# A three-pass fp32 backbone step: tanh gates, first sums on VectorE, and a pipeline for the right rows of two norms

## The chip, the cores and the metric

One core of a Trainium2 chip. The metric is the device time of one execution in microseconds (us), as the median of several runs. The engines named below are TensorE (PE in profile rows, PEld for its weight loads), VectorE (DVE), ScalarE (ACT), GpSimd (POOL) and SyncE (SP), whose queue starts most DMAs. Each engine works through its own queue in order.

## The reference

One layer of a diffusion backbone, for 128 context tokens and 512 latent tokens, width 1024, SwiGLU width 2816, four mLSTM heads of 256:

```python
mod = silu(cond) @ w_mod + b_mod
sh1, sc1, g1, shm, scm, gm, sh2, sc2, g2 = split(mod, 9)
h = modulate(rmsnorm(x, norm_g[0]), sh1, sc1)
x = x + 0.5 * g1 * swiglu(h, ffn1_w1, ffn1_w2)        # (silu(a) * b) @ w2
h = modulate(rmsnorm(x, norm_g[1]), shm, scm)
y, C, n, m = mixer(h, ...)
x = x + gm * y
h = modulate(rmsnorm(x, norm_g[2]), sh2, sc2)
x = x + 0.5 * g2 * swiglu(h, ffn2_w1, ffn2_w2)
...
# mixer
z = h @ w_in + b_in
q, k, v = heads of z;  o = sigmoid(z[O])
hm = mlstm_bidir(q, k, v, i, f, state)                # chunks of 128 tokens, two directions
hm = hm * rsqrt(mean(hm * hm) + EPS) * ml_norm
ml = (o * hm) @ w_ml_out
sc = (b * conv3(c * x)) @ w_sc_out
y = sigmoid(z[GML]) * ml + sigmoid(z[GSC]) * sc
return y @ w_o, C, n, m
```

At the end comes one more RMSNorm. `modulate(h, sh, sc)` is `h * (1 + sc) + sh`.

## The kernel before

**Products.** Activations are kept transposed (features on partitions), the 640 tokens in two halves of 320. Each fp32 product is three products of rounded parts, hi·hi, hi·lo and lo·hi (`three`, L240 to L242). `split` (L72 to L74) makes the parts: ScalarE casts hi, VectorE subtracts it to leave lo. Weights arrive by SyncE's DMAs (`w_load`, L197) in a ring of five raw tiles (`wr`).

**Pairs.** Most weights are used two tiles of 128 columns at a time, against the two halves of the tokens, by a form of Strassen's product with seven products instead of eight (`pair_el`, `pair_steps`). It goes through A11, S1, S2, A12, S3, S4, A22 in that order, and each meets activations of its own: H11, HT1, HT2, H21, HT3, H22, HT4. S1 to S4 are sums and differences of weight tiles (`ws`, L213): S2 and S4 are always VectorE's, S1 and S3 are those of the engine `e1`. Ahead of the last product, VectorE at L289 takes a copy of the accumulator plus the S1 product, since A22 (against HT4) then goes on adding in the same accumulator: HT4's first product waits for L289. A queue of casts runs four operations ahead of TensorE. In the first feed-forward part's first three pairs, `e1` is GpSimd.

**Norms and heads.** The last group of the matmuls ahead of norm two (ffn1's second product) and norm three (the mixer's output product) adds to the residual x (`add_x`, L844), squares it on ScalarE (L713), and VectorE adds the squares up in `sqacc` (L717). Half 0 of the tokens (the left rows) is then normalised while half 1 is still worked on: `left_lists` deals out, after each step of that group, lists of small works: `sc_` (scale by the norm, `scale_x`, VectorE, L760), `md` (`modulate`, L768 on ScalarE or L770 on VectorE), `sp` (`split` into H11 for k=0 to 3 and H21 for k=4 to 7). k counts the eight 128-row tiles of the width.

`head_el` then runs the next matmuls' first three column blocks on half 0, tile by tile: k=0 to 3 with H11, 4 to 7 with H21. Between them stands the statistics of half 1 (the right rows), made by `right_chain`: `chain[0]` sums the squares over partitions (L735), takes root and reciprocal and puts the result on a diagonal (L745); `chain[1]` spreads it (L752) and scales and modulates; `chain[2]` and `chain[3]` modulate and split the rest. Between the halves stand a few adaLN units (L561). Half 1 then reads HT4 for k=0 to 3 (a tile that the pairs use for something else later) and H22 for k=4 to 7.

**Gates.** Gate o is made in `q_pair` (L1325), per head; gml in `gml_pair` (L1532), for the first branch (mLSTM), and is written out by a GpSimd DMA; gsc, for the second branch, at L1655. All are Sigmoid on ScalarE. The attention weights between them use Exp (`w_exp`, L1344). Where two neighbouring functions are in different tables, an ACT_TABLE_LOAD stands between them. `r_out` (L1479) multiplies the transposed mLSTM output by ml_norm and o and writes it to DRAM (`rd`); `r_in` reads it and splits it (Bh, Bl); `ml_ev` (L1633) multiplies the first branch's product by gml, and `sc_ev` (L1673, L1674) the second's by gsc, and adds the two. In the scan, L1370, L1391 and L1437 are ScalarE's copies, L1407 scales an output, and the context state Cc goes out by DMA.

Orders are static: the program's order on each engine is the order of execution.

Of the kernel before, what the change touches and what calls it, by code (L numbers as in the profile page):

```python
# [7 lines left out]
F32 = mybir.dt.float32  # L8
# [4 lines left out]
P = 128  # L13
# [31 lines left out]
def mixer_step(ctx: ExitStack, tc: tile.TileContext, x_prompt, x_sample, state_C, state_n, state_m,  # L45
# [285 lines left out]
    def head_el(blocks, chain, work, mid=()):  # L331
# [7 lines left out]
        def emit():  # L339
# [22 lines left out]
            for k in range(KT):  # L362
                if k == 4:
                    for t in range(3):
                        w[t].append(op())
                for t in range(3):
                    three(ps[t][:, :HT], *w[t][k // 4], k % 4, plain_acts(k, 0), k == 0, k == KT - 1)
                if k == 3:
                    chain[0]()
                if k == 4:  # L370
                    chain[1]()
# [404 lines left out]
    def left_lists(n, sh):  # L776
        sc_ = lambda *ks: [lambda k=k: scale_x(0, k, N["rb", 0]) for k in ks]
        md = lambda *ks: [lambda k=k: modulate(0, k, n, sh, "AAV"[k % 3]) for k in ks]
        sp = lambda *ks: [lambda k=k: put("11" if k < 4 else "21", k % 4, N[0, k]) for k in ks]
        return [[stat_fn(0)], [rows_fn(0)] + sc_(0, 1, 2), sc_(3, 4) + md(0, 1), sc_(5, 6) + md(2) + sp(0),  # L780
                sc_(7) + md(3, 4) + sp(1, 2), md(5, 6) + sp(3, 4), md(7) + sp(5, 6, 7)]

# [11 lines left out]
    def right_chain(n, sh):  # L794
# [6 lines left out]

        def scales():
            for k in range(KT):
                scale_x(1, k, N["rb", 1])

        def mods(ks):
            for k in ks:
                modulate(1, k, n, sh, "AV"[k % 2])

        def right(ks):  # L810
            for k in ks:
                if k < 4:
                    HB.setdefault("12", [None] * 4)[k] = hl = hpair("T4")
                    split(N[1, k], *hl)
                else:
                    put("22", k - 4, N[1, k])

# [10 lines left out]
        def t4(k):  # L828
# [6 lines left out]
        last = [lambda k=k: put("T4", k, N["T", k]) for k in ks]  # L835
        chain = [stat_fn(1), all_of(rows_fn(1), scales, lambda: mods(range(4))),
                 all_of(lambda: mods(range(4, 8)), lambda: right(range(4))), lambda: right(range(4, 8))]
        return chain + last, work

# [57 lines left out]
    def after_lists(n, sh):  # L897
        lists = left_lists(n, sh)

        def after(h, i):  # L900
            if h == 1:
                for f in lists[i]:
                    f()
                if i == 5:
                    for f in lists[6]:
                        f()
        return after
# [200 lines left out]
    ptr["cap"] = 0  # L1108
    head, els = ffn(ffn1_w1, ffn1_w2, G1, after_lists(1, SHM), first_head, G)
    prog += [head] + with_units(els[0][0], mod_units(G1)) + [step(lambda: relax(0)), step(half_gate(G1))]  # L1110
# [200 lines left out]
    def q_pair(h, nm_, off):  # L1311
        S = HD[h]

        def ev(mi, hf, src):
            col0 = off + h * DH + mi * P
            if hf == 0 or (nm_, mi) not in S:
                if nm_ in "qk":
                    S[nm_, mi] = xp.tile([P, T], F32, name="x", bufs=KT)
                else:
                    S[nm_, mi] = PO["h1"].tile([P, T], F32, name=nm_, bufs=2)  # L1320
            dst = S[nm_, mi][:, hsl(hf)]
            if nm_ == "k":
                V.tensor_scalar(dst, src, bias(col0), DH ** -0.5, op0=OP.add, op1=OP.mult)
            else:
                A.activation(dst, src, AF.Sigmoid if nm_ == "o" else AF.Identity, bias=bias(col0))  # L1325
        return z_load(off + h * DH), z_load(off + h * DH + P), ev
# [20 lines left out]
    def head_steps(h):  # L1347
# [122 lines left out]
        def r_out(dt):  # L1470
            def f():
                j = 2 * h + dt
                for c0, c1 in ((0, 2), (2, NCH)):
# [4 lines left out]
                    o = S["o", dt][:, a:a + n]  # L1478
                    V.scalar_tensor_tensor(o, p[:, :n], col("ml", j), o, op0=OP.mult, op1=OP.mult)  # L1479
                G.dma_start(rd[j], S["o", dt])  # L1480
# [48 lines left out]
    def gml_pair(m):  # L1529
        def ev(mi, h, src):  # L1530
            t = t3()
            A.activation(t, src, AF.Sigmoid, bias=bias(GML_OFF + (m + mi) * P))  # L1532
            G.dma_start(gd[m + mi][:, hsl(h)], t)
        return z_load(GML_OFF + m * P), z_load(GML_OFF + (m + 1) * P), ev
# [3 lines left out]
    def cx_pair(m):  # L1538
        def ev(mi, h, src):
# [25 lines left out]
            for o, i in segs:  # L1565
# [6 lines left out]
                        mod_mid(GM, 0)))  # L1572
    prog += [step(spill_x), step(close_u), step(open_h1)]
    gate, NG = gates(), 38
# [40 lines left out]
    def r_in(j):  # L1615
        def f():
            for h in range(2):
                RB[j, h] = bpair()
                split(RT[j][:, hsl(h)], *RB[j, h])
        return f  # L1620
# [9 lines left out]
    def ml_ev(m):  # L1630
        def ev(h, ps):
            t = GM_T[m][:, hsl(h)]
            V.tensor_mul(t, ps, t)  # L1633
            if h == 1:
                G.dma_start(td[m], GM_T[m])
# [196 lines left out]
```

## Time and profile before

| | before |
|---|---|
| runs, us | 1711.39, 1711.75, 1712.96; median 1711.75 |
| profiled execution | 1712.5, of it span 1710.7 |
| busy, share of the span | TensorE 98%, VectorE 74%, ScalarE 47%, GpSimd 10% |
| mean granted TensorE clock | 0.997 |
| 0 to about 165 us | adaLN, norm one, ffn1's first pairs |
| 492 to 519 us | norm two and the mixer's head |
| 606 to 870 us | the scan and the gates o and gml |
| 1256 to 1280 us | norm three and ffn2's head |

A row of the timeline reads: start, duration, engine, line, operation, output <- inputs, shape, and in brackets how long the engine had been idle and what ended that. A row of groups ends with busy time and mean ns of one, then the idle time ahead of it. A row of waits gives total, times and longest.

### The profile page before, as it was taken

To read this page: it belongs to the slowest core of one execution; us is meant where nothing else is said; L and a number is where in the kernel's file an instruction comes from. 1 tells how busy PE (TensorE), PEld (TensorE's weight loads), DVE (VectorE), ACT (ScalarE), POOL (GpSimd) and SP (SyncE) were. 2 spreads that over 40 slices of the span, in tenths; PEclk is the share of its full clock that TensorE was granted. 3 is DMA by queue.
4 is the path that set the end of the run, shared out by engine and by line. 5 is a ranking of instruction groups with operands and counts; after the bars stand their busy time and mean duration, and the time that the engine had idled before them with its cause. 6 is when DMAs were issued, how large, how long until landed. Compare 5 with 4: busy or idle time off the path is not lost.

```text
span 1710.7 us, 29505 instructions
## 1 busy us (share of the span) xinstructions
PE 1669.3 (98%) x11275; PEld 1622.8 (95%) x11275; DVE 1268.8 (74%) x2677; ACT 798.4 (47%) x1719; POOL 166.3 (10%) x250
## 2 busy tenths in 40 slices
PE   7999999999999899999999999999999999999998
PEld 4979999999989899999999999999989999999997
DVE  6757786886778867777887788869677567567476
ACT  4542452542556666465652355542265335245243
POOL 2010000000030231111111212011100000000002
PEclk9999999999999999999999999999999999999999
DMA  9344334333352443333348423357432322323221
GB/s 310 87 150 135 99 110 122 109 109 107 106 155 75 107 105 84 84 100 83 94 140 265 131 75 87 95 164 215 132 99 65 97 62 84 91 75 87 87 75 62
DMA packets 277245, 193.14 MB, mean 113 GB/s; under 512 B 12147, under 2 KB 255226, under 8 KB 277104
## 3 DMA queue, kind: packets, MB, share of 16 engines
q1 hardware_dynamic: 268592, 162.62, 33.0%
q0 software_dynamic: 8480, 28.63, 6.0%
q8 instruction: 89, 1.46, 0.4%
q14 instruction: 52, 0.43, 0.1%
q10 hardware_dynamic: 32, 0.01, 0.0%
HBM read 175.92 MB, written 15.31 MB: 112 GB/s over the span
## 4 chain that ended last, share of the span: by engine, by line
PE 83%; DVE 8%; ACT 5%; issue 3%; DMA 1%; POOL 0%; ACTq 0%; DVEq 0%; POOLq 0%
PE ps L240 25%; PE ps L242 25%; PE ps L241 25%; DVE wl L74 2%; PE ax L1401 1%; PE ax L1432 1%; ACT wh L73 1%; PE ax L636 1%; PE ax L1404 1%; DVE ws L213 1%; DVE t L1545 1%; DMA wr<-in_ffn_w_dram 1%; PE ax L561 0%; DVE x L1557 0%; PE ax L1378 0%
## 5 line engine op out<-in xcount | busy, mean ns | idle before, releaser
L74 DVE TENSOR_TENSOR wl<-wr,wh 128x512 fp32r<-128x512 f32 (+1 forms) x410 | 268.1, 669 | 80.4 <-ACT wh L73 78.7
L73 ACT CAST wh<-wr 128x512 fp32r<-128x512 f32 (+1 forms) x410 | 238.6, 593 | 181.7 <-PE ps L241 152.6
L74 DVE TENSOR_TENSOR wl<-ws,wh 128x512 fp32r<-128x512 f32 x288 | 202.5, 704 | 62.8 <-ACT wh L73 62.4
L73 ACT CAST wh<-ws 128x512 fp32r<-128x512 f32 x288 | 175.2, 618 | 112.6 <-DVE ws L213 66.0
L240 PE MATMUL ps<-Uh,wh 128*128 128x320 f32 x704 | 218.8, 311 | 0.0
L241 PE MATMUL ps<-Ul,wh 128*128 128x320 f32 x704 | 217.6, 309 | 0.0
L242 PE MATMUL ps<-Uh,wl 128*128 128x320 f32 x704 | 217.4, 309 | 0.0
L844 DVE SCALAR_TENSOR_TENSOR x<-ps,modT,x 128x128 f32<-128x128 f32 (+2 forms) x216 | 82.8, 434 | 121.0 <-PE ps L242 121.0
L240 PE MATMUL ps<-HT4h,wh 128*128 128x320 f32 x384 | 122.0, 318 | 10.8 <-DVE t L289 4.5
L241 PEld LDWEIGHTS ps<-Ul,wh 128*128 128x128 f32 x704 | 132.3, 188 | 0.2 <-DVE Ul L74 0.2
L240 PEld LDWEIGHTS ps<-Uh,wh 128*128 128x128 f32 x704 | 132.3, 188 | 0.0
L242 PEld LDWEIGHTS ps<-Uh,wl 128*128 128x128 f32 x704 | 132.3, 188 | 0.0
L240 PE MATMUL ps<-H11h,wh 128*128 128x320 f32 x384 | 121.4, 316 | 2.0 <-ACT H11h L73 2.0
L240 PE MATMUL ps<-H21h,wh 128*128 128x320 f32 x384 | 120.4, 314 | 1.2 <-ACT H21h L73 1.2
L241 PE MATMUL ps<-H11l,wh 128*128 128x320 f32 x384 | 119.3, 311 | 0.6 <-DVE H11l L74 0.4
L241 PE MATMUL ps<-HT4l,wh 128*128 128x320 f32 x384 | 119.3, 311 | 0.2
L242 PE MATMUL ps<-H21h,wl 128*128 128x320 f32 x384 | 119.2, 311 | 0.3
L242 PE MATMUL ps<-HT4h,wl 128*128 128x320 f32 x384 | 119.2, 311 | 0.0
L241 PE MATMUL ps<-H21l,wh 128*128 128x320 f32 x384 | 118.9, 310 | 0.1
L242 PE MATMUL ps<-H11h,wl 128*128 128x320 f32 x384 | 118.8, 309 | 0.0
L240 PE MATMUL ps<-H22h,wh 128*128 128x320 f32 x352 | 110.3, 313 | 0.0
L242 PE MATMUL ps<-H22h,wl 128*128 128x320 f32 x352 | 109.0, 310 | 0.0
(401 smaller groups left out, 4528.2 us busy)
## 6 DMA issues: line engine op xcount, KB each, us to landing
wr<-in_ffn_w_dram SPq DMA_DIRECT2D x86, 512.0 KB, 4.0
wr<-in_w_in_dram SPq DMA_DIRECT2D x72, 512.0 KB, 3.9
wr<-in_w_mod_dram SPq DMA_DIRECT2D x64, 512.0 KB, 4.0
wr<-in_ffn_w_dram SPq DMA_DIRECT2D x48, 384.0 KB, 3.5
wr<-in_ffn_w_dram SPq DMA_DIRECT2D x20, 256.0 KB, 3.3
early<-in_w_mod_dram SPq DMA_DIRECT2D x8, 512.0 KB, 8.4
wr<-in_w_ml_out_dram SPq DMA_DIRECT2D x8, 512.0 KB, 5.2
wr<-in_w_sc_out_dram SPq DMA_DIRECT2D x8, 512.0 KB, 4.7
```

The costliest lines, as they stand in the source:

```text
L73: A.copy(hi, raw)
L74: V.tensor_sub(lo, raw, f32(hi))
L213: getattr(engine, fn)(t, part(o, a), part(o, b))
L240: PE.matmul(ps, hi[:, ws], ah, start=start, stop=False, skip_group_check=True)
L241: PE.matmul(ps, hi[:, ws], al, start=False, stop=False, skip_group_check=True)
L242: PE.matmul(ps, lo[:, ws], ah, start=False, stop=stop, skip_group_check=True)
L636: PE.matmul(p[:, 2 * j + i:2 * j + i + 1], hold_[i][j * P // n][:, a:a + P], ones[:, 0:1], start=True, stop=True)
L844: V.scalar_tensor_tensor(X[m][:, o + a:o + b], ps[:, a:b], modT[:, g, m, cd:cd + 1], X[m][:, o + a:o + b], op0=OP.mult, op1=OP.add)
L1401: PE.matmul(p2[:, :DH + 1], S["q", dt][:, sl], S["C"][d][:, dt, :], start=(dt == 0), stop=(dt == 1))
L1404: PE.matmul(p1[:, :DH + 1], S["p", ch][:, d, :], PO["vt"][:, ch, :], start=True, stop=True)
L1432: PE.matmul(p[:, :DH + 1], kw[:, dt * P:(dt + 1) * P], PO["vt"][:, ch, :], start=True, stop=True)
L1545: V.scalar_tensor_tensor(u, src, bias(X_OFF + m * P), u, op0=OP.add, op1=OP.mult)
```

## The change

Three things are changed.

1. ffn1's first three pairs make S1 and S3 on VectorE.
2. Gates o and gml are computed as tanh of half the argument, since sigmoid(z) is (1 + tanh(z/2))/2. The halved biases, and a halved ml_norm, are made once (`halve`, three small operations on VectorE). The 1 + is folded into operations that are there: `r_out` computes (o + 1)·p, `ml_ev` (t + 1)·ps, and `sc_ev` halves the first branch as it adds. ml_norm moves from `r_out` to `r_in`, where the cast becomes a Copy with a scale by partition and the subtraction a scalar_tensor_tensor. gsc stays a Sigmoid.
3. In the heads behind norms two and three, the left rows' splits move ahead of the next modulates, the last list (modulate 7, split 5, 6, 7) moves into the head behind k=1, the statistics of half 1 from behind k=3 to behind k=1, their spreading from behind k=4 to behind k=3. The right rows go through scale, modulate (now all on ScalarE) and split row by row, where before all scales came first, then all modulates, then all splits.

```diff
-                if k == 3:
-                    chain[0]()
-                if k == 4:
+                if k == 1:
+                    chain[0]()
+                    for f in N.pop("rest"):
+                        f()
+                if k == 3:
                     chain[1]()
...
-                sc_(7) + md(3, 4) + sp(1, 2), md(5, 6) + sp(3, 4), md(7) + sp(5, 6, 7)]
+                sc_(7) + sp(1) + md(3) + sp(2) + md(4), sp(3) + md(5, 6) + sp(4), md(7) + sp(5, 6, 7)]
...
+        def rows(k0, k1):
+            for k in range(k0, k1):
+                if k < KT:
+                    scale_x(1, k, N["rb", 1])
+                if 1 <= k <= KT:
+                    modulate(1, k - 1, n, sh)
+                if k >= 2:
+                    right(k - 2)
...
-        chain = [stat_fn(1), all_of(rows_fn(1), scales, lambda: mods(range(4))),
-                 all_of(lambda: mods(range(4, 8)), lambda: right(range(4))), lambda: right(range(4, 8))]
+        chain = [stat_fn(1), all_of(rows_fn(1), lambda: rows(0, 6)), lambda: rows(6, 9), lambda: rows(9, 10)]
...
-    head, els = ffn(ffn1_w1, ffn1_w2, G1, after_lists(1, SHM), first_head, G)
+    head, els = ffn(ffn1_w1, ffn1_w2, G1, after_lists(1, SHM), first_head)
...
+        for q, src in ((HO, biT[:, 24:32]), (HG, biT[:, 56:64]), (HM, vT[:, rows["ml"]:rows["ml"] + KT])):
+            V.tensor_scalar(halves[:, q], src, 0.5, None, op0=OP.mult)
...
-                A.activation(dst, src, AF.Sigmoid if nm_ == "o" else AF.Identity, bias=bias(col0))
+            elif nm_ == "o":
+                A.activation(dst, src, AF.Tanh, scale=0.5, bias=halves[:, HO, 2 * h + mi:2 * h + mi + 1])
...
-                    V.scalar_tensor_tensor(o, p[:, :n], col("ml", j), o, op0=OP.mult, op1=OP.mult)
+                    V.scalar_tensor_tensor(o, o, 1.0, p[:, :n], op0=OP.add, op1=OP.mult)
...
-            A.activation(t, src, AF.Sigmoid, bias=bias(GML_OFF + (m + mi) * P))
+            A.activation(t, src, AF.Tanh, scale=0.5, bias=halves[:, HG, m + mi:m + mi + 1])
...
-                split(RT[j][:, hsl(h)], *RB[j, h])
+                raw_, g = RT[j][:, hsl(h)], halves[:, HM, j:j + 1]
+                A.activation(hi, raw_, AF.Copy, scale=g)
+                V.scalar_tensor_tensor(lo, raw_, g, f32(hi), op0=OP.mult, op1=OP.subtract)
...
-            V.tensor_mul(t, ps, t)
+            V.scalar_tensor_tensor(t, t, 1.0, ps, op0=OP.add, op1=OP.mult)
...
-            V.tensor_add(t, t, g)
+            V.scalar_tensor_tensor(t, t, 0.5, g, op0=OP.mult, op1=OP.add)
```

What this does to the queues at four places. In the fences a row is a line of the program, the operation, its output and inputs, and the shape.

VectorE's queue around L289 of ffn1's first pair, where the second pair's weights are already made ready, before (`ws<-ws,wr` is the second pair's S2, `wl<-ws,wh` S1's lo, `wl<-wr,wh` A11's lo, and Ul the lo part of a SwiGLU output):

```order
L74 TENSOR_TENSOR wl<-wr,wh 128x512
L74 TENSOR_TENSOR Ul<-t_759,Uh 128x320
L213 TENSOR_TENSOR ws<-ws,wr 128x512
L74 TENSOR_TENSOR wl<-ws,wh 128x512
L289 TENSOR_TENSOR t_1201<-ps,t_1122 128x320
```

and now, with S1 (`ws<-wr`) at its head:

```order
L213 TENSOR_TENSOR ws<-wr 128x512
L74 TENSOR_TENSOR wl<-wr,wh 128x512
L74 TENSOR_TENSOR Ul<-t_760,Uh 128x320
L213 TENSOR_TENSOR ws<-ws,wr 128x512
L74 TENSOR_TENSOR wl<-ws,wh 128x512
L289 TENSOR_TENSOR t_1202<-ps,t_1123 128x320
```

S1 comes into the queue ahead of A11's lo and Ul, which stood first before.

ScalarE's queue at the end of ffn1's last group, ahead of norm two, from one square of the residual to the next, before:

```order
L713 ACTIVATE t_5764<-x 128x320
L768 ACTIVATE Uh<-Uh,modT,gcol 128x128
L768 ACTIVATE Uh<-Uh,modT,gcol 128x192
L768 ACTIVATE Ul<-Ul,modT,gcol 128x128
L768 ACTIVATE Ul<-Ul,modT,gcol 128x192
L73 CAST H11h<-Uh 128x320
L73 CAST H11h<-Ul 128x320
L713 ACTIVATE t_5795<-x 128x320
```

and now:

```order
L715 ACTIVATE t_5765<-x 128x320
L73 CAST H11h<-Uh 128x320
L770 ACTIVATE Uh<-Uh,modT,gcol 128x128
L770 ACTIVATE Uh<-Uh,modT,gcol 128x192
L73 CAST H11h<-Ul 128x320
L770 ACTIVATE Ul<-Ul,modT,gcol 128x128
L770 ACTIVATE Ul<-Ul,modT,gcol 128x192
L715 ACTIVATE t_5796<-x 128x320
```

The cast of the left rows' second tile (H11h<-Uh) moved from behind four modulate parts to a place ahead of them, and the third's ahead of the last two.

ScalarE's queue in the mixer's head, from the right rows' modulates on, before:

```order
L768 ACTIVATE Ul<-Ul,modT,gcol 128x320 x2
L1325 ACTIVATE x<-ps,biT 128x320 x2
L768 ACTIVATE Ul<-Ul,modT,gcol 128x320 x2
L73 CAST HT4h<-Ul 128x320
L73 CAST HT4h<-Uh 128x320
L73 CAST HT4h<-Ul 128x320
```

and now:

```order
L770 ACTIVATE Ul<-Ul,modT,gcol 128x320
L770 ACTIVATE Uh<-Uh,modT,gcol 128x320
L73 CAST HT4h<-Ul 128x320
L770 ACTIVATE Ul<-Ul,modT,gcol 128x320
L73 CAST HT4h<-Uh 128x320
L770 ACTIVATE Uh<-Uh,modT,gcol 128x320
L73 CAST HT4h<-Ul 128x320
L770 ACTIVATE Ul<-Ul,modT,gcol 128x320
```

Modulates and casts of one row after another now alternate, where two batches of modulates stood ahead of the first cast.

ScalarE's queue at head 0 of the scan, before:

```order
L73 CAST wh<-wr 128x512
L1532 ACT_TABLE_LOAD
L1532 ACTIVATE t_7140<-ps,biT 128x320
L1344 ACT_TABLE_LOAD
L1344 ACTIVATE wt<-wt,colT 128x128 x2
L73 CAST wh<-ws 128x512
L1344 ACTIVATE wt<-wt,colT 128x128 x2
L1370 COPY vt<-ax 128x256
L73 CAST wh<-ws 128x512
L1532 ACT_TABLE_LOAD
```

and now:

```order
L73 CAST wh<-wr 128x512
L1543 ACTIVATE t_7144<-ps,halves 128x320
L1355 ACTIVATE wt<-wt,colT 128x128 x2
L73 CAST wh<-ws 128x512
L1355 ACTIVATE wt<-wt,colT 128x128 x2
L1381 COPY vt<-ax 128x256
L73 CAST wh<-ws 128x512
L1543 ACTIVATE t_7204<-t_7095,halves 128x320
```

The table loads around the gate (L1532, now L1543) and the weights (L1344, now L1355) are no longer there.

More of the change, by code (lines that the diff above doesn't have):

```diff
@@ L800, in all_of, with right @@
             return f
[L802 to L816, printed above, removed]
+        def right(k):
+            if k < 4:
+                HB.setdefault("12", [None] * 4)[k] = hl = hpair("T4")
+                split(N[1, k], *hl)
+            else:
+                put("22", k - 4, N[1, k])
+        def rows(k0, k1):
[6 more added lines that the diff above has]
+                    right(k - 2)
         def t1(k):
@@ L904, in after @@
                 if i == 5:
-                    for f in lists[6]:
-                        f()
+                    N["rest"] = lists[6]
         return after
@@ L1136, in mixer_step, with halve @@
     nout = cst.tile([P, 16], F32, name="nout")
+    halves = cst.tile([P, 3, KT], F32, name="halves")
+    HO, HG, HM = range(3)
+    def halve():
+        for q, src in ((HO, biT[:, 24:32]), (HG, biT[:, 56:64]), (HM, vT[:, rows["ml"]:rows["ml"] + KT])):
+            V.tensor_scalar(halves[:, q], src, 0.5, None, op0=OP.mult)
     E_C, WK_C, WI_C, EN_C = range(4)
@@ L1323, in ev @@
                 V.tensor_scalar(dst, src, bias(col0), DH ** -0.5, op0=OP.add, op1=OP.mult)
+            elif nm_ == "o":
+                A.activation(dst, src, AF.Tanh, scale=0.5, bias=halves[:, HO, 2 * h + mi:2 * h + mi + 1])
             else:
-                A.activation(dst, src, AF.Sigmoid if nm_ == "o" else AF.Identity, bias=bias(col0))
+                A.activation(dst, src, AF.Identity, bias=bias(col0))
         return z_load(off + h * DH), z_load(off + h * DH + P), ev
@@ L1572, in mixer_step @@
                         mod_mid(GM, 0)))
-    prog += [step(spill_x), step(close_u), step(open_h1)]
+    prog += [step(spill_x), step(close_u), step(halve), step(open_h1)]
     gate, NG = gates(), 38
@@ L1617, in f @@
             for h in range(2):
-                RB[j, h] = bpair()
-                split(RT[j][:, hsl(h)], *RB[j, h])
+                hi, lo = RB[j, h] = bpair()
+                raw_, g = RT[j][:, hsl(h)], halves[:, HM, j:j + 1]
+                A.activation(hi, raw_, AF.Copy, scale=g)
+                V.scalar_tensor_tensor(lo, raw_, g, f32(hi), op0=OP.mult, op1=OP.subtract)
         return f
```

## The prediction

> **What bounds the kernel now.** I read the page's first part, then what TensorE waits for, then a table of stretches, and then the rows around each wait that the change touches.
>
> ```profile
> PE 1669.3 (98%) x11275; PEld 1622.8 (95%) x11275; DVE 1268.8 (74%) x2677; ACT 798.4 (47%) x1719; POOL 166.3 (10%) x250
> ...
> PE ps L240 <- DVE t L289: 4.5, 3, 2.0
> ...
> PE ps L240 <- ACT HT4h L73: 2.8, 2, 1.7
> ...
> PE ps L240 <- ACT H11h L73: 2.0, 2, 1.5
> ```
>
> TensorE is busy for 1669.3 of 1710.7 us, so 41 us of waits are all that a change without fewer matmuls can take, apart from the clock. The wait rows (total, times, longest) show three that lie in the places this change edits: L289's add, and the casts of a right row (HT4h) and a left row (H11h) of a norm.
>
> ```profile
> 94.22:97.63 3.41, 1.73 (x12) 1.00 0.45 150
> 111.29:114.70 3.41, 1.41 (x11) 1.00 0.34 120
> 114.70:118.12 3.42, 3.42 (x18) 0.50 0.00 0
> 170.00:480.00 310.00, 310.00 (x2135) 1.00 0.38 108
> ```
>
> The columns are the stretch, its length, TensorE's busy time and count, the granted clock, the DMA share and GB/s. The last row is the kernel's pace where nothing waits: 310/2135 = 0.145 us a matmul. The first three show the other loss: the stretch of 3.41 us that holds the 2.0 us wait is only 1.41 us busy, and the clock in the next 3.42 us is half. A stretch with 1.73 us busy was followed by no drop.
>
> **First pairs' sums.** S1 and S3 go from GpSimd to VectorE.
>
> ```profile
> 92.38 2.53 POOL L213 TENSOR_TENSOR ws<-wr 128x512 f32<-128x512 f32 x2 [35.94 <-DMA wr<-in_ffn_w_dram]
> ...
> L213 DVE TENSOR_TENSOR ws<-ws,wr x72: 674/685/1765, 69.7 to 1648.2; 128x512 f32<-128x512 f32 x72
> ...
> 93.70 1.76 DVE L213 TENSOR_TENSOR ws<-ws,wr 128x512 f32<-128x512 f32 x1 [1.80 <-POOL ws L213]
> 95.39 0.68 DVE L74 TENSOR_TENSOR wl<-ws,wh 128x512 fp32r<-128x512 f32 x1
> 95.99 0.48 DVE L289 TENSOR_TENSOR t<-ps,t 128x320 f32<-128x320 f32 x1
> ...
> 96.52 0.42 PE L240 MATMUL ps<-HT4h,wh 128*128 128x320 f32 x1 [1.69 <-DVE t L289]
> ...
> 113.83 0.42 PE L240 MATMUL ps<-HT4h,wh 128*128 128x320 f32 x1 [2.00 <-DVE t L289]
> ...
> 99.30 0.31 PE L241 MATMUL ps<-H11l,wh 128*128 128x320 f32 x1
> ...
> 118.07 0.34 PE L241 MATMUL ps<-H11l,wh 128*128 128x320 f32 x1
> ```
>
> The second pair's load lands at 92.38, while TensorE ends the first pair; GpSimd takes 2.53 us for both sums, and S2 on VectorE starts only after S1 and then runs 1.76 us instead of its median 0.685, for as long as GpSimd is at S3. From 95.39 to 95.99 a 512-wide operation costs VectorE's queue 0.60; by the same overlap of 0.08 a 320-wide one costs 0.40. After the change VectorE's queue is: S1 from 92.38, A11's lo (which now stands behind S1 and waits for the load with it), Ul, S2, S1's lo, L289: 92.38 + 4×0.60 + 0.40 = 95.18, end 95.66 in place of 96.47. That is 0.81 off the wait of 1.69. Behind the waiting S1 in VectorE's queue stand A11's lo and one Ul; both are used after the last product HT4 only, so TensorE doesn't feel them. The wait of 2.00, where the third pair's load lands, loses 0.79 by the same walk. The first pair's own sums lie in VectorE's idle time and I cost them at nothing; if that cover is gone they cost 2×0.60. The two remaining waits (0.88, 1.21) are the load's.
>
> With 1.2 us of wait, that stretch is 2.2 us busy, more than the 1.73 that was followed by full clock, so I take the drop as gone. Its price: the same instructions, first HT4 to second H11l, took 99.30−96.52 = 2.78 us at full clock and 118.07−113.83 = 4.24 in the drop, 1.46 more. Sum of the part: 0.81+0.79+1.46 = **3.06**. Bounds: 0.8 (the third pair's load does not come earlier, and the drop stays) and 3.7+1.5 (both waits gone).
>
> [...]
>
> **Norm two, in the mixer's head.**
>
> ```profile
> 500.07 0.42 PE L240 MATMUL ps<-H11h,wh 128*128 128x320 f32 x1 [1.54 <-ACT H11h L73]
> ...
> 497.93 0.92 ACT L768 ACTIVATE Uh<-Uh,modT,gcol 128x128 f32<-128x128 f32 x2
> ...
> 499.58 0.44 ACT L73 CAST H11h<-Uh 128x320 fp32r<-128x320 f32 x1
> ...
> 500.86 0.54 DVE L844 SCALAR_TENSOR_TENSOR x<-ps,modT,x 128x320 f32<-128x320 f32 x1
> 502.07 0.49 DVE L717 TENSOR_TENSOR sqacc<-sqacc,t 128x320 f32<-128x320 f32 x1 [0.67 <-ACT t L713]
> ...
> 505.00 0.39 PE L735 MATMUL ax<-ones,sqacc 128*128 128x2 f32 x3
> ...
> 508.48 0.39 PE L240 MATMUL ps<-H21h,wh 128*128 128x320 f32 x1
> ...
> L768 ACT ACTIVATE Ul<-Ul,modT,gcol 128x320 f32<-128x320 f32 x8 | 5.0, 651 | 5.6 <-DVE Ul L760 5.3
> ...
> 514.73 0.42 PE L240 MATMUL ps<-HT4h,wh 128*128 128x320 f32 x1 [1.05 <-ACT HT4h L73]
> ...
> 518.73 0.31 PE L240 MATMUL ps<-HT4h,wh 128*128 128x320 f32 x1
> ```
>
> The cast of row 1 (499.58) stood behind two modulates from 497.93; now it stands ahead of them, 1.65 earlier, and k=1's products start at 498.4 instead of 500.07. But the sums of squares (L735) now stand behind k=1, not k=3, and need the last sqacc. That comes from the x at 500.86, whose queue moves up by some 0.86 only (one cast and one lo less ahead of it), so it ends at 501.7. TensorE, done with k=1 at 500.1, gets a new wait of about 1.6: the first wait is not removed, it moves. Then nothing waits until L752: its diagonal takes 3.1 us from L735 (505.00 to 508.1 before), so 504.8 to 505.0, which k=2 and 3 fill (18×0.145 = 2.6). With L752's 0.6 and k=4's nine products (1.3) k=5 starts at 507.0, against 508.48: 1.5 earlier.
>
> The eight right rows then go through in a pipeline, ScalarE at 0.55 for a modulate (0.65 less overlap; before it had four of the eight) and 0.36 for a cast (0.45 less overlap), 0.95 us a row with a little for the hand-over, while TensorE needs 0.44 (three products). HT4's first row is ready at about 508.5; TensorE wants it at 507.0+5.2 = 512.2, so the wait of 1.05 goes. Its lead of 3.7 us is eaten at 0.5 a row: the last of the H22 rows are 0.4 to 0.8 late. The first unit's half ends at 516.45, where 518.73 stood: 2.28; I take **2.0**, since each small wait has a restart too (0.42 against 0.31 for the matmul after a wait). Bounds: 0 (the sqacc wait takes all) and 2.9 (both waits, with restarts).
>
> **Norm three, in ffn2's head.** The same edit.
>
> ```profile
> 1259.05 0.49 DVE L717 TENSOR_TENSOR sqacc<-sqacc,t 128x320 f32<-128x320 f32 x1 [0.67 <-ACT t L713]
> ...
> 1261.98 0.39 PE L735 MATMUL ax<-ones,sqacc 128*128 128x2 f32 x3
> ...
> 1268.87 1.28 ACT L870 ACT_TABLE_LOAD   x1 [1.15 <-PE ps L242]
> ...
> 1272.40 0.41 PE L240 MATMUL ps<-HT4h,wh 128*128 128x320 f32 x1 [1.74 <-ACT HT4h L73]
> ```
>
> L735 behind k=1 would be reached at 1261.98−18×0.145 = 1259.4; sqacc, moved up like in norm two, is there at about 1258.6, so here there is no new wait. The wait of 1.74 for HT4h goes, with 0.8 of waits ahead of it; but the Silu table's 1.28 us at 1268.87 now stands between rows of the pipeline, and the H22 rows come 0.8 to 1.1 late. I take **1.8**; bounds 0.7 (the table load and the pace take more) and 2.6.
>
> **Gates.**
>
> ```profile
> L1344 ACT ACT_TABLE_LOAD x5 | 6.4, 1283 | 0.1
> L1532 ACT ACT_TABLE_LOAD x4 | 5.1, 1283 | 0.8 <-PE ps L242 0.8
> ...
> 618.82 1.28 ACT L1532
> ...
> 622.24 0.48 PE L1432 MATMUL ax<-vt,kw 128*128 128x257 f32 x1 [0.50 <-ACT vt L1370]
> ...
> 635.25 0.33 PE L1388 MATMUL ax<-ident,x 128*128 128x128 f32 x1 [0.90 <-ACT t L1407]
> ...
> 836.61 1.28 ACT L1325
> ...
> 847.11 0.44 PE L1388 MATMUL ax<-ident,x 128*128 128x128 f32 x2 [0.93 <-ACT t L1407]
> ```
>
> Tanh and Exp need no change of table between them, so of the loads at L1344, L1532 and L1325 all go but the first; 1.28 us each. Five of them stand from 606 to 619, on a chain that TensorE feels twice (0.50 and 0.90); the load at 618.82 is a link of the chain that ended last. With 6.4 us off that chain both waits go, with 0.07 for restarts, and the rest of the 6.4 was hidden: **1.47**. Late next is the round trip of the state by DMA that follows, which starts earlier with them. The load at 836.61 is a link too, and VectorE's and ScalarE's queue behind it is full up to the wait of 0.93 at 847.11; that wait and its restart go: **1.1**. The other loads I cost at nothing: TensorE has no wait between 640 and 830, nor does it get one. Bounds: 0 and 1.4+1.3+0.5.
>
> **Losses.**
>
> ```profile
> L73 ACT CAST Bh<-x 128x320 fp32r<-128x320 f32 x32 | 13.8, 455 | 11.7 <-DVE x L1641 9.4 <-DMA x<-rd 2.1 <-issue 0.2
> ...
> L1407 ACT ACTIVATE t<-ax,colT 128x257 f32<-128x257 f32 x32 | 15.1, 472 | 15.7 <-PE ax L1401 15.7
> ```
>
> In r_in 16 casts become a Copy with a scale by partition; no row shows one at 320. It lies between L1407's 0.472 (257 wide, a scale by partition) and the modulate's 0.651, so +0.02 to +0.2; I take 0.09, nearer to L1407, and four of them stand on a path that TensorE waits on: −**0.4**. The 48 operations of VectorE that become SCALAR_TENSOR_TENSOR cost 0.54 against 0.49 (the two rows at 500.86 and 502.07), 2.4 us in all, beside matmuls, hidden while VectorE has a quarter of its time free; without that cover they cost the 2.4. The new load ahead of gsc costs 0 to 0.4, the three halvings −**0.1**.
>
> Sum: 3.06+2.0+1.8+1.47+1.1−0.4−0.1 = **8.9**. The profiled execution was 1712.5 (span 1710.7 and 1.8 around it), so 1703.6 on its level; the median of the runs, 1711.75, is 0.75 below it, so 1702.9, and I say **1703.0**. A measurement of this kernel can tell 0.2% from no change, 3.4 us.
>
> **Rivals.**
> 1. *The clock drop stays or moves.* [...] Then 1.46 is not gained: 1704.5. The same comes if a wait of 2.0 never caused the drop. Against both: the drop followed the emptier of the two stretches shown at once. Chance 0.17. [...]
> 2. *The loads set place one.* If the third pair's load lands when it did, L289's gain there is nothing and the gap stays: part one is 0.8: 1705.3. For it: VectorE waited for that load. Chance 0.12.
> 3. *The table loads were hidden.* If what follows Cc (a round trip by DMA) sets both places, 2.6 is not gained: 1705.6. Against: the chain names the loads. Chance 0.08. With the second as well, 1708.
> 4. *Slower: the right rows go in lockstep.* All eight modulates on ScalarE, each waiting for VectorE's scale and waited for by VectorE's lo, could make a row as long as the four steps one after the other: 0.49+0.65+0.45+0.49 = 2.1 us. To be slower by 3.4 the norms must lose 5.1+3.4 = 8.5 together, 4.3 each, which puts the end of norm two's half at 523.0: from the first scale at 507.3 that is 1.9 us a row (eight rows and the fill). At 2.1: 1716. Against: each queue has the next row's scale ahead of the lo that waits, so no step needs the row after it. Chance 0.04.
> 5. *The norms give nothing,* since the sqacc wait eats norm two and the table norm three: 3.8 less, 1706.8; with rival one 1708.3. Chance 0.09.
>
> **The numbers.** My forecast has 0.5; its own range is 1701 to 1705. With cases one, two, three and most of five the range reaches 1708.5; Below, if all of the edited waits go (3.06+2.9+2.6+1.4+1.1+0.5 for restarts, no losses: 11.6) it is 1700.2, with half a microsecond for the spread of the runs 1699.5. The two ends leave out 0.2. The time is faster by over 0.2% below 1708.3. All cases but the fourth lie there alone (0.96); two and three together, or five and one with losses above my sum, reach the band of no change: 0.09. So faster 0.87, same 0.09, slower 0.04.
>
> **What would show it.** Right: L289's waits at 0.9 and 1.2 and no half clock near 115; a wait ahead of L735 of about 1.6 in norm two and none in norm three; no wait for HT4h in either head, small ones for H22h; no table loads at L1532 and L1344's line but one; no wait for t L1407 near 635 and 847. Wrong: an L289 wait still near 2.0, H22h waits of over 1 us a row, or the wait at 635 merely named otherwise.

## The result, and the profile after

The changed kernel takes 1700.2 us (median of four runs, 1698.9 to 1701.15), against 1711.57 (1711.01 to 1712.96) for the kernel before beside it: 11.4 us less, a ratio of 0.9932 with a 95% interval of 0.9915 to 0.9949. The forecast was 1703.0, between 1699.5 and 1708.5. The profiled execution took 1700.71, its span 1698.9. The page's first part, and what TensorE waits for (total, times, longest):

```profile
PE 1667.4 (98%) x11275; PEld 1623.4 (96%) x11275; DVE 1267.9 (75%) x2678; ACT 790.9 (47%) x1716; POOL 158.4 (9%) x244
...
PE ps L240 <- DVE t L289: 2.1, 3, 1.0
...
PE ax L737 <- DVE sqacc L719: 1.2, 3, 0.9
...
PE ps L241 <- DVE H11l L74: 1.0, 2, 0.6
```

The casts of HT4h and H11h in the two heads are gone from the list, and so are L1388 and L1432 of the scan. New are two smaller waits in norm two: for the last sum of squares and for a left row's lo part. The windows (stretch, length, TensorE's busy time and count, granted clock, DMA share, GB/s) of this profile:

```profile
495.42:498.83 3.41, 2.02 (x13) 1.00 1.05 319
498.83:502.24 3.41, 3.41 (x15) 0.50 1.03 417
17.55:20.96 3.41, 3.29 (x15) 0.50 1.06 389
111.29:114.70 3.41, 3.16 (x26) 1.00 0.30 105
```

Near 115 the clock is full now. But there is half clock in two other places, for 3.41 us each: right behind norm two's new waits, and at the start, where the kernel before had none in its profile. Such a stretch of 3.41 us, at half clock or full, is called a window below.

The rows of the first place and of norm two:

```profile
94.61 0.69 DVE L213 TENSOR_TENSOR ws<-ws,wr 128x512 f32<-128x512 f32 x1
...
95.82 0.49 DVE L289 TENSOR_TENSOR t<-ps,t 128x320 f32<-128x320 f32 x1
...
96.36 0.41 PE L240 MATMUL ps<-HT4h,wh 128*128 128x320 f32 x1 [0.99 <-DVE t L289]
...
111.92 0.42 PE L240 MATMUL ps<-HT4h,wh 128*128 128x320 f32 x1 [0.25 <-DVE t L289]
...
494.43 0.44 ACT L73 CAST H11h<-Uh 128x320 fp32r<-128x320 f32 x1
...
494.90 0.98 DVE L74 TENSOR_TENSOR H11l<-Uh,H11h 128x320 fp32r<-128x320 f32 x1 [0.56 <-ACT H11h L73]
...
498.25 0.94 PE L737 MATMUL ax<-ones,sqacc 128*128 128x2 f32 x6 [0.88 <-DVE sqacc L719]
```

S2 takes 0.69 us with GpSimd idle, and L289 ends 3.31 behind the landing of the load (93.00); by the walk of the prediction it was 3.28. Of the 22 loads of tables (1.283 us each) 12 are gone and one is new (L1668, ahead of gsc). At the attention weights' Exp (now L1355) none is left of five, and at gml (now L1543) one of four.

To see what each place gave, I took the time between the starts of the same two matmuls of TensorE's queue, in every profile of this study. "Old" are profiles of kernels with that place as before, "new" as in the change. The stretches are named by the times of the kernel before.

| stretch, us | old | new |
|---|---|---|
| 0 to 60, start (not changed) | 60.0 to 62.7 in all | |
| 94 to 99.3, first L289 | 5.36, 5.48, 5.46; 6.42 with half clock | 4.45 to 4.66 |
| 99.3 to 124, second L289 | 22.13, 22.64, 22.76; 24.66 with half clock (before) | 21.20 to 21.67 |
| 490 to 521, norm two | 30.95, 30.98, 31.11 | 28.67 to 28.70; 29.87, 29.88, 29.88 with half clock |
| 521 to 576 (not changed) | 54.95 to 54.97 in all, with half clock near 560 or without | |
| 603 to 640, gates, first part | 36.90, 36.84, 36.76 | 34.20 in every one |
| 830 to 850, gates, last head | 19.93, 19.94, 19.95 | 18.79 (18.81) |
| 885 to 905, x<-rd and r_in | 19.98 (before), 19.49, 18.76, 18.24 | 18.73 (after), 18.39 to 18.91; 19.39 in the second profile |
| 1250 to 1282, norm three | 31.93, 31.93; 33.46 with half clock | 30.24 to 30.39 |

### The profile page after: what moved, and what is told of

Its sections match the earlier page's. It is cut to its first block, busy times and chain, and to the rows that moved or that the text cites. A ratio compares the mean times of both kernels' runs of the same rounds, so it can differ in the third digit from the quotient of the medians.

```text
span 1698.9 us, 29486 instructions
## 1 busy us (share of the span) xinstructions
PE 1667.4 (98%) x11275; PEld 1623.4 (96%) x11275; DVE 1267.9 (75%) x2678; ACT 790.9 (47%) x1716; POOL 158.4 (9%) x244
## 3 DMA queue, kind: packets, MB, share of 16 engines
q8 instruction: 89, 1.46, 0.4%
## 4 chain that ended last, share of the span: by engine, by line
PE 85%; DVE 8%; ACT 3%; issue 3%; DMA 1%; POOL 0%; ACTq 0%; DVEq 0%; POOLq 0%
PE ps L240 26%; PE ps L241 25%; PE ps L242 25%; DVE wl L74 2%; PE ax L1443 2%; PE ax L1412 2%; PE ax L638 1%; PE ax L1415 1%; ACT wh L73 1%; PE ax L563 1%; DVE ws L213 1%; DVE t L1556 1%; PE ax L1389 1%; DMA wr<-in_ffn_w_dram 0%; DVE x L1568 0%
## 5 line engine op out<-in xcount | busy, mean ns | idle before, releaser
L241 PE MATMUL ps<-H22l,wh 128*128 128x320 f32 x352 | 109.1, 310 | 0.4
```

The source lines that it names most:

```text
L241: PE.matmul(ps, hi[:, ws], al, start=False, stop=False, skip_group_check=True)
```

## Experiments

### Each part alone

The first pairs' sums alone (the call of `ffn` for ffn1 without `G`, nothing else):

> Only the first pairs' sums S1 and S3 move to VectorE; norms and gates as before. Theory (the L289 waits are made of VectorE's and GpSimd's work after the load, and the half clock near 115 follows the emptier window): the first L289 wait falls from 1.69 to about 0.9, the second from 2.00 to 0.3 to 1.2, no half clock between 110 and 120, 3 to 4 us less than before: about 1708. Rival (the load sets the place, and the clock drop comes whatever the gap): the second wait stays near 2.0 or the drop stays, 0.8 to 1.6 us less: about 1710.

1709.33 us (11 runs, 1706.8 to 1710.77) against 1711.67: 2.3 less, ratio 0.9985 (0.9976 to 0.9994), between the two theories. The waits for L289 are 0.85 and 0.51, as the first had it, and there is no half clock at 115. But there is at 498.2, and behind norm three's still old wait:

```profile
494.78:498.20 3.42, 1.76 (x10) 1.00 0.92 252
498.20:501.61 3.41, 3.41 (x15) 0.50 1.04 388
...
1266.19:1269.61 3.42, 1.57 (x12) 1.00 0.72 205
1269.61:1273.02 3.41, 3.41 (x15) 0.50 0.41 102
```

So the drop is not tied to the place, and its price is not fixed: norm three took 33.46 here and 31.93 in the two other old profiles, 1.53 more, but norm two only 31.11 against 30.95 and 30.98.

The heads' order alone (the hunks of `head_el`, `left_lists`, `right_chain`, `after_lists`):

> Only the order in the heads behind norms two and three changes; sums and gates as before. Theory: norm three gives 1.8; norm two gives 2.3 to 2.7 less the half-clock stretch that its new waits (sqacc 0.9, H11l 0.6) bring in some executions (1.45): together 2.9 to 4.3 us less than before, about 1708. In the profile no wait for HT4h, a wait of 0.9 ahead of L737, and, if the window falls so, half clock from there on. Rival (the drop in norm two belongs to the whole change's timing and not to the waits): norm two gives 2.3 or more with no drop at all, 4.1 or more together.

1705.9 us (1704.99 to 1706.86): 5.8 less, ratio 0.9967 (0.9955 to 0.998), more than the theory's 2.9 to 4.3; the rival had 4.1 or more. In its profile norm two has the same two waits as the changed kernel (0.60 and 0.89), and no half clock behind them: 28.70 against 30.95, 2.25 less. Norm three gives 1.66. The second profile of the changed kernel (below) has these waits without half clock, too, so the drop does not belong to the whole change, as the rival had it. The places hold 3.9 of the 5.8. The interval reaches down to 3.4, so the rest may be scatter; the half clock that norm three's old wait brings in some executions (1.53) is another candidate, and how often it comes was not measured.

The gates alone (hunks of `q_pair`, `r_out`, `gml_pair`, `halve`, `r_in`, `ml_ev`, `sc_ev`):

> Only the tanh gates and what goes with them (halves, r_out, r_in, ml_ev, sc_ev); sums and norms as before. Theory (a wait that goes pays its idle time and its restart; the wait of 1.63 for a landing of x<-rd is cured with them): 2.6 near 606 to 636, 1.2 at 846, 1.3 near 897: about 5 us less, 1706.5. Rival (the wait near 897 comes and goes with the DMA's luck and has nothing to do with the gates): 3.5 to 3.8 us less, about 1708, and the wait for t L286 near 897 stands in this profile.

1707.8 us (nine runs, 1706.47 to 1709.27): 3.9 less, ratio 0.9979 (0.9969 to 0.9988): the rival's time. The stretches give 2.64 (603 to 640) and 1.14 (830 to 850), 3.8 together. The rival also expected the wait of 1.63 near 897 to stand in this profile, and it does not. But other profiles show that it comes with how long one x<-rd load, the fifth, takes to land. ScalarE's rows that wait for it, in the kernel before, with the sums alone and with the heads alone, all three with the old r_in:

```profile
897.11 0.82 ACT L73 CAST Bh<-x 128x320 fp32r<-128x320 f32 x2 [2.06 <-DMA x<-rd]
...
892.68 0.82 ACT L73 CAST Bh<-x 128x320 fp32r<-128x320 f32 x2 [1.04 <-DMA x<-rd]
...
891.89 0.82 ACT L73 CAST Bh<-x 128x320 fp32r<-128x320 f32 x2 [0.59 <-DMA x<-rd]
```

That load took 5.94, 4.93 and 4.48 us, and 4.58 in the kernel with the gates alone. A second profile of the changed kernel (below) shows a load of 5.52 and a wait for t L286 of 1.01 there, too. So the 1.25 that this stretch gave between the two first profiles is not the change's.

The change without the sums (the call with `G` again):

> The changed kernel with the first pairs' sums S1 and S3 on GpSimd as before: norms and gates alone. Theory (the parts lie 300 us and more apart and add up): it is 1.5 to 2.5 above the changed kernel, 1702 to 1703, as the sums alone gave 2.3 below the kernel before. Rival (the clock's windows tie the parts together): nearer than 1 us to the changed kernel, or more than 3.5 above it.

1702.47 us (1701.87 to 1705.61), 1.6 above the changed kernel run beside it (1700.88): that fits parts that add up, though the runs of the two overlap. Its waits for L289 are 1.79 and 1.59:

```profile
PE ps L240 <- DVE t L289: 4.2, 3, 1.8
```

The second wait was 2.00, 0.96, 0.89 and 1.59 in the four profiles with the old sums and at most 0.51 in the new ones.

### The clock

The changed kernel with L289's add repeated in every second pair:

```diff
-                    V.tensor_add(S["c22"], S["c"][:, :HT], S["p5"])
+                    PROBE["n"] += 1
+                    for _ in range(1 + PROBE["add"].get(PROBE["n"], 0)):
+                        V.tensor_add(S["c22"], S["c"][:, :HT], S["p5"])
...
+    PROBE = {"n": 0, "add": {n: 6 + (n // 2) % 5 for n in range(4, 80, 2)}}
```

> The changed kernel with L289's add issued 7 to 11 times in place of once in every second pair from the fourth on (30 places; the same values are written again), so that TensorE waits some 1 to 3 us ahead of HT4 there. [...]

1827.85 us in one run. Three of its waits, and the windows that hold them with the ones behind:

```profile
319.94 0.52 PE L240 MATMUL ps<-HT4h,wh 128*128 128x320 f32 x1 [1.97 <-DVE t L292]
...
1420.91 0.41 PE L240 MATMUL ps<-HT4h,wh 128*128 128x320 f32 x1 [3.55 <-DVE t L292]
...
1550.42 0.41 PE L240 MATMUL ps<-HT4h,wh 128*128 128x320 f32 x1 [2.51 <-DVE t L292]
...
316.68:320.10 3.42, 1.45 (x10) 1.00 0.00 0
320.10:323.51 3.41, 3.41 (x14) 0.50 0.00 0
...
1415.78:1419.19 3.41, 1.59 (x11) 1.00 0.42 115
1419.19:1422.61 3.42, 1.70 (x11) 1.00 0.00 0
1548.90:1552.31 3.41, 1.89 (x13) 1.00 0.03 7
1552.31:1555.73 3.42, 3.42 (x25) 1.00 0.36 108
```

The wait of 1.97 us lies inside one window (1.45 us busy), and the clock of the next is 0.50. The wait of 3.55 falls half into one window and half into the next (1.59 and 1.70 us busy), the one of 2.51 leaves 1.89 busy, and the clock stays 1.00. The nineteen half-clock stretches between 180 and 1660 us start a whole number of 3.4133 us apart, to 0.002. Worked out for each window of that grid from 180 to 1690 us: all 19 windows at full clock with 1.57 us of matmuls or less were followed by half clock; of the 24 with 1.59 to 2.71 one was (1.73). So in this profile the half clock goes with how little of one window was busy and not with the length of the wait alone.

The changed kernel once more:

> The changed kernel once more, for comparison on the same chip and for a second profile. [...] Rival (the drop in norm two belongs to the change): half clock from about 498.8 again.

1700.88 us (1700.22 to 1702.98). Norm two is at full clock (28.68), and the half clock stands behind a wait near 560 that the change doesn't touch:

```profile
495.20:498.61 3.41, 2.59 (x15) 1.00 0.92 276
559.24:562.65 3.41, 1.57 (x11) 1.00 0.47 152
562.65:566.06 3.41, 3.41 (x15) 0.50 0.00 0
```

The grid lies otherwise in each of these executions: its first line is 2.06 us behind the span's start in the kernel before (half clock from 114.70), 0.48 in the first profile of the changed kernel (from 498.83) and 2.86 in this one (from 562.65). Near 560 the half clock costs nothing: in the five profiles that have it there, the wait for t L292 behind it is 0.12 to 0.14 in place of 1.66, and the stretch from 521 to 576 takes 54.95 to 54.97 with it and without.

Outside the probe the edge is less sharp. From 80 us on, windows with 1.56 to 1.59 us of matmuls were followed by half clock and most with 1.69 to 2.1 were not. But the 1.76 of the kernel with the sums alone was (shown above, 128x320 matmuls only), and so were the 1.94 to 2.02 ahead of norm two's half clock in three profiles of the new order, where L737's two-column matmuls count as busy. So the profile's busy time alone does not tell which windows have half clock behind them; what does was not shown.

### The heads

Statistics behind k=2 and spreading behind k=4 in the mixer's head:

```diff
-                if k == 1:
+                if k == at[0]:
                     chain[0]()
...
-                if k == 3:
+                if k == at[1]:
                     chain[1]()
...
-                        mod_mid(GM, 0)))
+                        mod_mid(GM, 0), (2, 4)))
```

> The whole change, but in the mixer's head the statistics of half 1 (and the deferred list) stand behind k=2 and their spreading behind k=4, where the change has them behind k=1 and k=3; ffn2's head as in the change. Theory (the changed kernel waits 0.9 for sqacc and then runs 3.41 us at half clock, both because the statistics come too early): no wait ahead of L737 in norm two, no half clock near 500, 1.4 to 2.3 us below the changed kernel, about 1698. Rival (the diagonal, 3 us behind the statistics, only waits elsewhere, or the right rows come too late for HT4): a wait of 1 us ahead of L754 or HT4h, within 0.6 us of the changed kernel, about 1700.

1700.47 us (1699.14 to 1701.39): the rival. The wait for sqacc is gone and there is no half clock near 500, but the stretch is 28.70, as with the wait and full clock. The spreading comes 0.2 us later than in the second profile of the change, and the H22 rows are what is late now; their first products restart three times (0.41 in place of 0.31):

```profile
511.10 0.41 PE L241 MATMUL ps<-H22l,wh 128*128 128x320 f32 x1
...
512.00 0.42 PE L241 MATMUL ps<-H22l,wh 128*128 128x320 f32 x1
...
513.06 0.41 PE L241 MATMUL ps<-H22l,wh 128*128 128x320 f32 x1
```

They stand 0.9 and 1.06 apart: that is the pipeline's pace, and it ends the head in both: from the same matmul ahead of norm two, the last of the three comes after 25.51 us here and after 25.50 in the second profile of the change.

The change with the right rows in batches as before (`right_chain` of the kernel before, with every second modulate on VectorE again):

> The changed kernel with the right rows of norms two and three in batches as before (all scales, all modulates, half of them on VectorE, all splits), but with the earlier left rows, the earlier statistics and the earlier spreading of the change. Theory (the earlier statistics carry the gain, since the first HT4 row came 6.5 us behind L752 in batches in norm two and 7.6 in norm three, and TensorE now comes to HT4 7.1 us behind it in both): norm two as in the change or up to 0.5 better, norm three 0.5 to 0.9 worse: within 0.6 us of the changed kernel, 1700.5. Rival (the pipeline takes the waits away): the waits of 1.05 and 1.74 for HT4h stand again, 2 to 3 us above the changed kernel.

1702.12 us (1701.19 to 1705.18) beside 1711.23 for the kernel before, 1.2 to 1.9 above the changed kernel's two medians (1700.88 and 1700.2), between the two theories. The rival is right on the waits: both stand again, at the old length, 1.05 and 1.74. ScalarE's rows in the mixer's head:

```profile
PE ps L240 <- ACT HT4h L73: 2.8, 2, 1.7
...
504.33 1.45 ACT L770 ACTIVATE Ul<-Ul,modT,gcol 128x320 f32<-128x320 f32 x2 [1.19 <-DVE Ul L762]
508.29 0.97 ACT L1336 ACTIVATE x<-ps,biT 128x320 f32<-128x320 f32 x2 [2.51 <-PE ps L242]
509.15 1.19 ACT L770 ACTIVATE Ul<-Ul,modT,gcol 128x320 f32<-128x320 f32 x2
510.24 0.45 ACT L73 CAST HT4h<-Ul 128x320 fp32r<-128x320 f32 x1
```

ScalarE had its first modulates done and then stood idle for 2.51 us at L1336, the emptying of the accumulators of half 0, with the other modulates and all casts behind it. So the wait for HT4h was never made by late statistics: the cast stood in line behind TensorE's own work, and earlier rows could not move it. Norm two takes 29.55 and norm three 30.84. Of the 2.25 and 1.67 that the heads give, the earlier rows and statistics make 1.4 and 1.1, the pipeline (with all modulates on ScalarE) 0.85 and 0.6.

The seventh tile's squares on VectorE, and S1 of the first pairs on GpSimd:

```diff
-            "S1": spec(total("S1", e1, "tensor_add", "A21", "A22"), r2),
+            "S1": spec(total("S1", e1 if e1 is not FIRST else G, "tensor_add", "A21", "A22"), r2),
...
-            (G if 1 < m < KT - 1 else V).tensor_add(sq["acc"][:, a:b], sq["acc"][:, a:b], t)
+            (G if 1 < m < KT - 2 else V).tensor_add(sq["acc"][:, a:b], sq["acc"][:, a:b], t)
```

(the first run has S1 alone; `FIRST` marks the first three pairs, whose S3 stays on VectorE.)

> The changed kernel with S1 of the first three pairs on GpSimd again and only S3 on VectorE. Theory (the waits for L289 have two parts in the kernel before: VectorE's S2 ran 1.76 us in place of 0.69 while GpSimd was at S3, and S1 on GpSimd is ready 1.3 us after the load; on VectorE, S1 brings A11's lo and one Ul behind the load instead): S2 takes 0.69 again, the queue is S2, S1's lo, L289 from 1.3 us behind the load, so L289 ends 2.9 us behind the load in place of 3.3: the first wait for L289 is 0.5 to 0.6 in place of 0.8 to 1.0, 0.3 to 0.7 us below the changed kernel. Rival (S1 on GpSimd is what made the waits): the waits are 1.7 and 0.9 again, 1.4 us above the changed kernel.

1701.12 us (1698.88 to 1701.8), not to be told from the changed kernel. The profile has the rows expected:

```profile
93.29 1.28 POOL L215 TENSOR_TENSOR ws<-wr 128x512 f32<-128x512 f32 x1 [37.46 <-DMA wr<-in_ffn_w_dram]
...
94.60 0.69 DVE L215 TENSOR_TENSOR ws<-ws,wr 128x512 f32<-128x512 f32 x1 [1.94 <-POOL ws L215]
...
95.87 0.48 DVE L291 TENSOR_TENSOR t<-ps,t 128x320 f32<-128x320 f32 x1
```

S2 takes 0.69, where it took 1.76 beside S3 on GpSimd; the add ends 3.06 behind the load in place of 3.31. The wait is 0.80, hardly less than 0.78 to 0.99.

> The kernel before it in this list, and the sums of squares of the seventh tile (k=6) on VectorE in place of GpSimd, in all norms. Theory (in norm two, one subtraction of H11l takes 0.98 in place of 0.49 while GpSimd adds squares, and TensorE waits 0.60 for it): that wait falls to 0.1 to 0.2, norm two 0.4 to 0.6 shorter; together 0.7 to 1.2 below the changed kernel, about 1699.3. Rival (the added operation delays VectorE as much as the conflict did): 0 from this part.

1700.71 us (1700.18 to 1701.47): the rival. The conflict is gone (0.48 in place of 0.98), but the add waits for its square and now stands ahead of the subtraction, with a scale behind it:

```profile
496.19 0.49 DVE L721 TENSOR_TENSOR sqacc<-sqacc,t 128x320 f32<-128x320 f32 x1 [0.67 <-ACT t L717]
496.60 0.48 DVE L764 TENSOR_TENSOR Uh<-x,ax 128x320 f32<-128x320 f32 x1
497.00 0.48 DVE L74 TENSOR_TENSOR H11l<-Uh,H11h 128x320 fp32r<-128x320 f32 x1
```

The wait is 0.63 and norm two 28.69.

### The gates

Gate o as a Sigmoid again, with the change otherwise:

```diff
-                A.activation(dst, src, AF.Tanh, scale=0.5, bias=halves[:, HO, 2 * h + mi:2 * h + mi + 1])
+                A.activation(dst, src, AF.Sigmoid, bias=bias(col0))
...
-                    V.scalar_tensor_tensor(o, o, 1.0, p[:, :n], op0=OP.add, op1=OP.mult)
+                    V.scalar_tensor_tensor(o, o, 2.0, p[:, :n], op0=OP.mult, op1=OP.mult)
```

> The changed kernel with gate o as a Sigmoid again (r_out multiplies it by 2), so that table loads stand at o again in each head; gml stays Tanh. Theory (what 606 to 640 gave came from gml's loads, what 830 to 850 gave from the load at o of the last head, and the loads at o of the heads between are hidden): 606 to 640 keeps its 34.2 us, 830 to 850 is 19.9 again, about 1.2 us more than the changed kernel, 1701.4. Rival (ScalarE's queue pays for every load): seven loads of 1.28 us, of which more than two show: 2.5 us or more above the changed kernel.

1704.1 us (four runs, 1701.54 to 1706.74), too wide for tenths. The stretches: 603 to 640 keeps its 34.20, 830 to 850 is back at 19.80. So the first part is gml's and the last the load at o. But 640 to 830 takes 191.9 in place of 190.2, with a new wait at head 1, so the loads at o ahead of the last head are not all hidden:

```profile
642.57 1.28 ACT L1334 ACT_TABLE_LOAD   x1
...
651.29 0.68 POOL L1349 TENSOR_TENSOR wt<-wt,mask 128x256 f32<-128x256 f32 x1
...
651.35 1.24 DVE L74 TENSOR_TENSOR wl<-ws,wh 128x512 fp32r<-128x512 f32 x1 [1.09 <-ACT wh L73]
...
657.52 0.42 PE L240 MATMUL ps<-HT2h,wh 128*128 128x320 f32 x1 [1.46 <-ACT ps L268]
```

The load at 642.57 starts it. Counted from the same matmul in this profile and the changed kernel's, L1418 starts 1.10 us later, VectorE's chain behind it carries 1.06 of that to the subtraction at 651.35, and that now runs beside GpSimd's L1349 and takes 1.24 in place of 0.69. ScalarE's copy at L268, for which TensorE waits, comes 1.48 later. The wait of 1.46 and the 0.27 of a restart (worked out below) make the 1.7.

r_in as a plain split, ml_norm in r_out:

```diff
                 A.activation(dst, src, AF.Tanh, scale=0.5, bias=halves[:, HO, 2 * h + mi:2 * h + mi + 1])
+                V.tensor_scalar(dst, dst, 0.5, 0.5, op0=OP.mult, op1=OP.add)
...
-                    V.scalar_tensor_tensor(o, o, 1.0, p[:, :n], op0=OP.add, op1=OP.mult)
+                    V.scalar_tensor_tensor(o, p[:, :n], col("ml", j), o, op0=OP.mult, op1=OP.mult)
...
-                hi, lo = RB[j, h] = bpair()
...
+                RB[j, h] = bpair()
+                split(RT[j][:, hsl(h)], *RB[j, h])
```

> The changed kernel with ml_norm left in r_out and r_in as a plain cast and subtraction; the tanh of o becomes a sigmoid by one more operation of VectorE (8 in all, 0.4 each). Theory (the Copy with a scale costs ScalarE 0.1 more than a cast on a path that TensorE waits for): the stretch that took 18.7 us in the changed kernel and 18.2 in the kernel with the norms alone (885 to 905 of before) takes 18.2 to 18.4, 0.4 below the changed kernel, 1699.8. Rival (that stretch is set by the landing of x<-rd, and the Copy is hidden): no difference, or 0.3 more by the added operations.

1702.08 us (1700.78 to 1703.62): inconclusive. The fifth x<-rd load took 5.74 us, and TensorE waited for t L286:

```profile
890.40 0.42 PE L240 MATMUL ps<-HT4h,wh 128*128 128x320 f32 x1 [1.43 <-ACT t L286]
```

The stretch took 19.49, so nothing is told of r_in's price, nor why this kernel was slower: another 0.6 lies between 640 and 830.

No version of these was clear of the changed kernel's 1700.2 to 1700.9.

## Why the prediction was right, and where it wasn't

The direction, the range and the main terms held, but the range only just: 1700.2 lies 0.7 above its low end and below the 1701 to 1705 that had half of the chance. The gain was 11.4 where 8.75 stood. In the terms, the sums' was some 1.1 too big and the gates' 1.4 too small; that these nearly cancel is luck. Point by point:

- **First pairs' sums, 3.06.** The first wait's 0.81 is 0.9 by the stretches. The second lost 1.75 and not 0.79 between the two profiles, since the load also took 4.1 us in place of 4.9; over all profiles it lost 1.1 (mean of 2.00, 0.96, 0.89 and 1.59 to 0.2). The price of a half-clock stretch, 1.46, was near at some places (1.53 at norm three, 1.19 in the new norm two); it was 0.15 in the old norm two and nothing near 560. The step that failed is taking it as gone: the first rival, that it moves, came about. In the changed kernel's first profile it stood at the start and in norm two, in the second at the start and near 560. What the sums alone give was 2.3.
- **Norm two, 2.0.** 2.25 at full clock, as the walk's 2.28, and 1.08 with the half clock of the profile after. The new wait ahead of the statistics came, as 0.88 in place of 1.6, with a wait of 0.60 for H11l that the walk lacked. TensorE doesn't wait for an H22 row there in the profile after, and 0.11 in the second, where 0.4 to 0.8 was reckoned with.
- **Norm three, 1.8.** 1.67; no new wait ahead of L737, as worked out.
- **Gates, 1.47 and 1.1.** The last head gave 1.14. The first part gave 2.56 to 2.70: the term "0.07 for restarts" was mis-sized. TensorE's rows around a wait in the kernel before:

```profile
94.53 0.31 PE L242 MATMUL ps<-H22h,wl 128*128 128x320 f32 x1
...
96.78 0.32 PE L241 MATMUL ps<-HT4l,wh 128*128 128x320 f32 x1
```

From the last matmul ahead of the wait (94.53) to the second behind it (96.78) 2.25 us passed, where two steps of 0.147 would have been 0.29: 1.96 lost, and the row lists 1.69. So this wait costs 0.27 more: 0.16 by which the last row ahead of it (0.31) is longer than a step, and 0.11 by which the first row behind it (0.42) is longer than that. The same working gives 0.26 to 0.27 at the ten other single waits above 0.25 between such matmuls in this profile. Three waits stood in the gates' stretch, 0.17, 0.50 and 0.90, 1.57 as listed and 2.4 in this way; between the two profiles the offset grows by 0.43, 0.77 and 1.11 at them. Some 0.3 more was lost at 612, where the offset also moves, without a listed wait.
- **Losses, 0.5.** The Copy takes 0.556 against 0.454 for the cast it replaces, 0.10 where the prediction took 0.09. ScalarE's groups, and a wait in that stretch, after:

```profile
L1631 ACT ACTIVATE Bh<-x,halves 128x320 fp32r<-128x320 f32 x16 | 8.1, 556 | 0.3 <-issue 0.2
...
L73 ACT CAST Bh<-x 128x320 fp32r<-128x320 f32 x16 | 7.3, 454 | 9.4 <-DVE x L1654 9.4
...
885.15 0.42 PE L240 MATMUL ps<-HT3h,wh 128*128 128x320 f32 x1 [0.53 <-ACT ps L278]
```

Where x<-rd brings TensorE no wait above 0.2 the stretch is 18.24 with the cast and 18.39 to 18.73 with the Copy, a loss of 0.15 to 0.49 by a single old profile. The loss has a place: in all nine profiles of kernels with the Copy, the gap probe aside, TensorE waits 0.25 to 0.53 for ps L278 there; with the cast it waited 0.23 in the kernel before and not at all in three others. A landing that was late in the profile before and not in the one after hid the loss: 1.25 the other way.
- **Rivals.** The first happened, without ending the gain. The second didn't: the load's landing moved with the work ahead of it. The third didn't: more of the table loads showed, not less. The fourth didn't: the rows went at 0.9 to 1.06 us, not 1.9. Nor did the fifth: the norms gave 3.9 at full clock.

The stretches without luck are 0.9+1.1 (sums), 2.25+1.67 (norms), 2.64+0.19+1.14 (gates, 0.19 from 576 to 603), less 0.15 to 0.49: 9.4 to 9.7. The second comparison gave 10.4 (1711.29 to 1700.88) where the first gave 11.4, so about 1 us of the difference is what comparisons scatter by. Fewer costly half-clock stretches are a candidate for the rest. Of the old places, the first L289 had one in one profile of four, the second in one of four, and norm three in one of three, at about 1.5 each (1.53 at norm three; 29.06 against 27.61 for both L289 stretches with nearly the same waits); the new norm two had one in three profiles of nine, at 1.19. That would be worth 0.9, an estimate from counts too small to lean on.

## What to carry to other kernels

A listed wait of TensorE between 128x320 matmuls costs its idle time and 0.27 us here, so several short ones are worth more than their sum. When a cast is late, look at what stands ahead of it in its own engine's queue before hurrying its inputs: here that was an evacuation of accumulators that kept ScalarE idle for 2.51 us, and earlier inputs did not help (waits of 1.05 and 1.74 as before). The half-clock stretches shown here stood behind windows with 1.41 to 2.02 us of matmuls in 3.41, and at other places in one execution than in the next; what a change wins by such a stretch is a chance and not a term. A table load that shows no wait near it can still show one 15 us later, through the chain that it delays, as the one at 642.57 did at 657.52.

## What the runs showed of the hardware that I had not expected

The grid of 3.4133 us on which the probe's half-clock stretches start, and an edge at 1.57 to 1.59 us of matmul time in a window (46%) in the probe, with one exception (1.73); elsewhere half clock stood behind up to 2.02. A wait of 1.84 us near 560, in every profile with the same length, had half clock behind it in five of them and none in the others, and the stretch around it took 54.95 to 54.97 us in all. A subtraction on VectorE took 0.98 us beside GpSimd's add of squares and 0.48 without it, and S2 took 1.76 beside GpSimd's S3 and 0.69 without it. One x<-rd load took 4.45 to 5.94 us to land in kernels that issue it in the same order.
